# Instance norm on one core: loops without a block, one activation table, and a first store that waits for the third load

## The chip, the cores and the metric

One core of a Trainium2 chip. The metric is the device time of one execution in microseconds, as the profiler takes it. It is 1.7 us longer than the span from the first to the last instruction.

## The reference

```python
x: (8, 64, 32, 64, 64) float32            # 512 instances of 131072 elements
mean = np.mean(x, axis=(2, 3, 4), keepdims=True)
var  = np.var(x, axis=(2, 3, 4), keepdims=True)
out  = (x - mean) / np.sqrt(var + eps)
```

268 MB are read and 268 MB are written; each element is needed once.

## The kernel before

Data moves in 64 tiles of 128 partitions x 8192 floats (4 MiB) through six slots. The last tile is handled as two halves. SyncE issues all loads, ACT issues all stores: one queue for each. A slot is loaded again when its store has landed. The six first loads are issued at once.

```python
def on_scalar(eng, t, lane, n, c1, c2, c16, dst):        # one tile on ACT
    eng.activation(..., func=Act.Identity, accum_out=a[:, 1:2])._wait_ge(landed[lane], c16)
    eng.activation(..., func=Act.Square, bias=a[:, 2:3], accum_out=a[:, 3:4])._wait_ge(centred[lane], c1)
    eng.activation(..., func=Act.Sqrt, bias=eps_t[:, 0:1])._wait_ge(varied[lane], c1)
    eng.activation(out=t[:, :w], func=Act.Identity, scale=a[:, 5:6], bias=a[:, 6:7])._wait_ge(shifted[lane], c1)
    eng.dma_start(out=dst, in_=t)._wait_ge(done[lane], c2).then_inc(stored[lane], 16)
...                                                       # VectorE and TensorE likewise
block = ctx.enter_context(nc.Block())

@block.sync
def _(eng):
    for s in range(SLOTS):
        eng.dma_start(out=slots[s][:], in_=x_t[s]).then_inc(landed[s], 16)
    ...
    with eng.Fori(1, ROUNDS) as it:
        for s in range(SLOTS):
            eng.dma_start(out=slots[s][:], in_=x_t[it * SLOTS + s])._wait_ge(stored[s], c16).then_inc(landed[s], 16)
...
@block.scalar
def _(eng):
    eng.wait_ge(ready, READY)
    over_tiles(eng, on_scalar, with_target=True)          # Fori of 10 passes x 6 tiles, then 5 more
    ...                                                   # ACT waits for all stores
```

## Time and profile before

| | before |
|---|---|
| time, median | 1248.55 us (1248.55, 1248.55, 1250.43) |
| span of the profiled run | 1246.9 us |
| DMA | 431 GB/s over the span, 433 in the middle |
| ACT / DVE busy | 79% / 38% |
| ACT_TABLE_LOAD | 20, two in each loop pass |
| first store issued | 31.85 us |

Read it as a kernel that moves bytes: the engines have slack, and whatever is not plain transfer lies in the first 41 us and the last 24. The lines are in the prediction.

### The profile page before, as it was taken

The page shows a single profiled execution, that of the slowest core. Times are in us where ns is not written, and L with a number is a line of the kernel's source. Part 1 is how long each engine was busy: PE and PEld are TensorE (multiplying, and loading weights), DVE is VectorE, ACT ScalarE, POOL GpSimd, SP SyncE. Part 2 cuts the span into 40 slices and gives each one's busy share as a digit, 9 for nine tenths or more (in the row PEclk, how much of TensorE's full clock was granted, in tenths as well). Part 3 has the DMA queues.
Part 4 walks back from the last instruction along what each step waited for, and adds up shares of the span by engine and source line. Part 5 has one row for each costly group of instructions (what it writes and reads, how often), then busy time and mean ns, then how long its engine had stood idle before and what let it go on. Part 6 is the DMA issues. An engine that isn't in the chain of part 4 may idle for free.

```text
span 1246.9 us, 1819 instructions
## 1 busy us (share of the span) xinstructions
PE 76.4 (6%) x260; PEld 65.2 (5%) x260; DVE 467.9 (38%) x325; ACT 986.1 (79%) x410; POOL 1.9 (0%) x11
## 2 busy tenths in 40 slices
PE   0000000000000000000000000000000000000000
PEld 0000000000000000000000000000000000000000
DVE  2344334433334334343343433433334333343331
ACT  5888888887787878778777878787787878778774
POOL 0000000000000000000000000000000000000000
DMA  9999999999999999999999999999999999999998
GB/s 403 422 435 427 433 436 435 428 433 436 435 428 433 437 434 429 432 436 435 431 430 436 436 434 425 437 436 435 427 434 436 435 428 433 436 435 428 433 432 376
DMA packets 18723, 536.90 MB, mean 431 GB/s; under 512 B 2081, under 2 KB 2081, under 8 KB 2081
## 3 DMA queue, kind: packets, MB, share of 16 engines
q1 hardware_dynamic: 9360, 268.44, 50.0%
q10 hardware_dynamic: 9360, 268.44, 49.9%
q14 instruction: 3, 0.02, 0.0%
HBM read 268.44 MB, written 268.44 MB: 431 GB/s over the span
## 4 chain that ended last, share of the span: by engine, by line
ACT 48%; DVE 29%; another core or an unknown queue 13%; PE 6%; issue 1%; DMA 1%; ACTq 0%; DVEq 0%; SPq 0%
ACT unused L113 37%; DVE small L79 18%; DVE slot L95 8%; ACT slot L123 4%; ACT unused L107 4%; PE psum L136 3%; PE psum L143 3%; ACT small L120 1%; ACT L120 1%; DMA slot<-in_x_dram 1%; DVE small L89 1%; DVE small L82 1%; DVE small L92 1%; ACTq L130 0%
## 5 line engine op out<-in xcount | busy, mean ns | idle before, releaser
L113 ACT ACTIVATE unused<-slot,small 128x8192 uint8<-128x8192 f32 (+1 forms) x65 | 456.1, 7017 | 90.1 <-DVE small L82 90.1
L79 DVE TENSOR_REDUCE small<-slot 128x1 f32<-128x4096 f32 (+1 forms) x65 | 282.9, 4353 | 164.4 <-DMA slot<-in_x_dram 164.4
L107 ACT ACTIVATE unused<-slot 128x4096 uint8<-128x4096 f32 (+1 forms) x65 | 231.7, 3564 | 82.1 <-DMA slot<-in_x_dram 77.0
L123 ACT ACTIVATE slot<-slot,small 128x4096 f32<-128x4096 f32 (+1 forms) x65 | 243.7, 3749 | 27.6 <-DVE small L92 27.6
L89 DVE RECIPROCAL small<-small 128x1 f32<-128x1 f32 x65 | 10.6, 164 | 533.8 <-ACT small L120 533.8
L95 DVE TENSOR_SCALAR slot<-slot,small 128x4096 f32<-128x4096 f32 (+1 forms) x65 | 154.7, 2379 | 2.4
L136 PE MATMUL psum<-small,avg 128*128 128x2 f32 x130 | 38.2, 363 | 674.1 <-DVE small L79 548.7
L136 PEld LDWEIGHTS psum<-small,avg 128*128 128x128 f32 x130 | 32.6, 311 | 679.6 <-DVE small L79 553.0
L143 PE MATMUL psum<-small,avg 128*128 128x1 f32 x130 | 38.2, 363 | 480.6 <-ACT unused L113 480.6
L143 PEld LDWEIGHTS psum<-small,avg 128*128 128x128 f32 x130 | 32.7, 312 | 486.2 <-ACT unused L113 486.2
L120 ACT ACTIVATE small<-psum,eps_t 128x1 f32<-128x1 f32 x65 | 17.0, 261 | 37.4 <-PE psum L143 37.3
L82 DVE TENSOR_REDUCE small<-psum 128x1 f32<-128x2 f32 x65 | 10.3, 159 | 62.5 <-PE psum L136 62.5
L107 ACT ACT_TABLE_LOAD x10 | 12.8, 1283 | 10.4 <-ACT slot L123 7.1
L120 ACT ACT_TABLE_LOAD x10 | 12.8, 1283 | 0.2
L107 ACT ACTIVATION_READ_ACCUMULATOR unused<-slot 128x1 f32 x65 | 12.1, 186 | 0.0
L113 ACT ACTIVATION_READ_ACCUMULATOR unused<-slot,small 128x1 f32 x65 | 12.1, 186 | 0.0
L92 DVE TENSOR_TENSOR small<-small 128x1 f32<-128x1 f32 x65 | 10.3, 159 | 2.2
L208 POOL TENSOR_SCALAR_AFFINE_SELECT avg<-avg 128x128 f32<-128x128 f32 x4 | 1.3, 324 | 0.3
L205 POOL MEMSET avg<- 128x128 f32 x2 | 0.4, 204 | 0.5 <-SPq L42 0.5
L257 POOL MEMSET const-bfloat16-1.0<- 128x1 bf16 x1 | 0.1, 101 | 0.0
L257 POOL MEMSET const-uint8-127<- 128x1 uint8 x1 | 0.1, 101 | 0.0
L257 POOL MEMSET const-float32-0.0<- 128x1 f32 x1 | 0.1, 98 | 0.3 <-issue 0.3
(2 smaller groups left out, 0.2 us busy)
## 6 DMA issues: line engine op xcount, KB each, us to landing
slot<-in_x_dram SPq DMA_DIRECT2D x63, 4096.0 KB, 52.8
out_dram<-slot ACTq DMA_DIRECT2D x63, 4096.0 KB, 45.3
slot<-in_x_dram SPq DMA_DIRECT2D x2, 2048.0 KB, 55.6
out_dram<-slot ACTq DMA_DIRECT2D x2, 2048.0 KB, 14.7
```

The source lines that it names most:

```text
L79: eng.reduce_sum(out=a[:, 0:1], in_=t[:, :w], axis=mybir.AxisListType.X)._wait_ge(landed[lane], c16).then_inc(summed[lane], 1)
L82: eng.tensor_reduce(out=a[:, 2:3], in_=psum[lane][:, 0:2], axis=mybir.AxisListType.X, op=Alu.add, negate=True,)._wait_ge(meaned[lane], c1) ...
L89: eng.reciprocal(out=a[:, 5:6], in_=a[:, 4:5])._wait_ge(rooted[lane], c1).then_inc(scaled[lane], 1)
L92: eng.tensor_mul(out=a[:, 6:7], in0=a[:, 2:3], in1=a[:, 5:6])._wait_ge(scaled[lane], c1).then_inc(shifted[lane], 1)
L95: eng.tensor_scalar(out=t[:, w:], in0=t[:, w:], scalar1=a[:, 5:6], scalar2=a[:, 6:7], op0=Alu.mult, op1=Alu.add,)._wait_ge(shifted[lane], ...
L107: eng.activation(out=unused[:, w : 2 * w], in_=t[:, w:], func=Act.Identity, accum_out=a[:, 1:2],)._wait_ge(landed[lane], c16).then_inc(sum ...
L113: eng.activation(out=unused[:, : 2 * w], in_=t, func=Act.Square, bias=a[:, 2:3], accum_out=a[:, 3:4],)._wait_ge(centred[lane], c1).then_in ...
L120: eng.activation(out=a[:, 4:5], in_=psum[lane][:, 2:3], func=Act.Sqrt, bias=eps_t[:, 0:1])._wait_ge(varied[lane], c1).then_inc(rooted[lane ...
L123: eng.activation(out=t[:, :w], in_=t[:, :w], func=Act.Identity, scale=a[:, 5:6], bias=a[:, 6:7],)._wait_ge(shifted[lane], c1).then_inc(don ...
L136: eng.matmul(out=psum[lane][:, 0:2], lhsT=avg[n][:], rhs=a[:, 0:2], start=True, stop=True,)._wait_ge(summed[lane], c2).then_inc(meaned[lan ...
L143: eng.matmul(out=psum[lane][:, 2:3], lhsT=avg[n][:], rhs=a[:, 3:4], start=True, stop=True,)._wait_ge(squared[lane], c1).then_inc(varied[la ...
L208: eng.affine_select(out=m[:], in_=m[:], pattern=[[sign * split, n], [0, split]], compare_op=Alu.is_ge, fill=0.0, base=0 if sign < 0 else s ...
```

## The change

The intent: no block, so no entry and exit of one; one activation table loaded ahead, in place of two switches in each loop pass; the first store held until the third load has landed. "Last tile in two halves" is in both kernels.

```diff
+    FIRST_BEHIND = 2
...
+        if lane == 0:
+            eng.wait_ge(landed[FIRST_BEHIND], 16)
         eng.dma_start(out=dst, in_=t)._wait_ge(done[lane], c2).then_inc(stored[lane], 16)
...
-    block = ctx.enter_context(nc.Block())
-    @block.sync
-    def _(eng):
+    def load_all(eng):
...                                            # SyncE now waits for all stores, ACT no longer
+        for lane in range(LANES):
+            eng.wait_ge(stored[lane], 16 * uses)
...
+    load_all(nc.sync)
+    set_by = set_up(nc.gpsimd)
+    over_tiles(nc.vector, on_vector)
+    nc.tensor.wait_ge(ready, set_by)
+    over_tiles(nc.tensor, on_tensor)
+    nc.scalar.preload_act_table(Act.Sqrt)
+    nc.scalar.wait_ge(ready, set_by)
+    over_tiles(nc.scalar, on_scalar, with_target=True)
```

More of the change, by code (lines that the diff above doesn't have):

```diff
@@ L160 @@
         rest.append((x_h[k], out_h[k], half, SLOTS + h, 1, FULL // 2))
+    MATRICES = [(m, n, 1.0 / n_elem) for n, m in avg.items()]
     def over_tiles(eng, step, with_target=False):
@@ L197, in _, with set_up @@
             )
-    @block.gpsimd
-    def _(eng):
+        for lane in range(LANES):
+            uses = sum(1 for r in rest if r[3] == lane) + (ROUNDS if lane < SLOTS else 0)
+            eng.wait_ge(stored[lane], 16 * uses)
+    def set_up(eng):
         count = 0
-        for n, m in avg.items():
+        for m, n, value in MATRICES:
             split = P // n
-            eng.memset(m[:], 1.0 / n_elem).then_inc(ready, 1)
+            eng.memset(m[:], value).then_inc(ready, 1)
             count += 1
@@ L218, in _ @@
         eng.memset(eps_t[:], eps_f).then_inc(ready, 1)
-    READY = 3 * len(avg) + 1
-    @block.vector
-    def _(eng):
-        over_tiles(eng, on_vector)
-    @block.tensor
-    def _(eng):
-        eng.wait_ge(ready, READY)
-        over_tiles(eng, on_tensor)
-    @block.scalar
-    def _(eng):
-        eng.wait_ge(ready, READY)
-        over_tiles(eng, on_scalar, with_target=True)
-        for s in range(SLOTS):
-            uses = ROUNDS + sum(1 for r in rest if r[3] == s)
-            eng.wait_ge(stored[s], 16 * uses)
-        for s in range(SLOTS, LANES):
-            eng.wait_ge(stored[s], 16)
+        return count + 1
+    load_all(nc.sync)
[6 more added lines that the diff above has]
+    over_tiles(nc.scalar, on_scalar, with_target=True)
 _INS = ['x', 'eps']
```

## The prediction

> **What bounds the kernel now.** I first read the page, by slices, then the groups, to see whether an engine or the DMA sets the time:
>
> ```profile
> span 1246.9 us, 1819 instructions
> PE 76.4 (6%) x260; PEld 65.2 (5%) x260; DVE 467.9 (38%) x325; ACT 986.1 (79%) x410; POOL 1.9 (0%) x11
> ...
> DMA  9999999999999999999999999999999999999998
> HBM read 268.44 MB, written 268.44 MB: 431 GB/s over the span
> ```
>
> The DMA row is 9 in 39 of 40 slices, and ACT, the busiest engine, is idle a fifth of the time. The chain that ended last names ACT for 48%, but that chain follows releases backwards and does not say what is full. I therefore cut the span into stages. The columns are stretch, its length, busy time of PE, PEld, DVE, ACT and POOL, clock, DMA share, GB/s:
>
> ```profile
> 0.00:2.05 2.05, 0.00 (x0) 0.00 (x0) 0.00 (x0) 0.00 (x0) 1.09 (x8) 1.00 0.00 0
> 2.05:31.50 29.45, 1.18 (x4) 1.01 (x4) 8.38 (x6) 17.23 (x8) 0.80 (x4) 1.00 1.01 427
> 31.50:41.20 9.70, 0.59 (x2) 0.50 (x2) 3.42 (x2) 8.35 (x4) 0.00 (x0) 1.00 1.02 402
> 41.20:116.20 75.00, 5.28 (x18) 4.51 (x18) 30.45 (x23) 64.34 (x28) 0.00 (x0) 1.00 1.00 432
> 116.20:1180.90 1064.70, 65.20 (x222) 55.71 (x222) 407.44 (x278) 854.27 (x352) 0.00 (x0) 1.00 1.00 433
> 1180.90:1223.40 42.50, 2.94 (x10) 2.51 (x10) 14.07 (x13) 33.73 (x16) 0.00 (x0) 1.00 1.00 432
> 1223.40:1243.20 19.80, 1.17 (x4) 1.00 (x4) 4.11 (x5) 8.16 (x6) 0.00 (x0) 1.00 0.98 423
> 1243.20:1245.40 2.20, 0.00 (x0) 0.00 (x0) 0.00 (x0) 0.00 (x0) 0.00 (x0) 1.00 0.05 22
> 1245.40:1246.90 1.50, 0.00 (x0) 0.00 (x0) 0.00 (x0) 0.00 (x0) 0.00 (x0) 1.00 0.00 0
> ```
>
> From 2 us to 1243 us the DMA engines are full, at 433 GB/s for the long middle. All 536.9 MB at 433 GB/s are 1239.9 us, so only about 7.0 us of the span are not plain transfer. The table says where they lie, each as length x (1 - rate/433): 2.05 before the first packet, 0.41 in the ramp, 0.69 in the stage where the first store joins the loads (31.5 to 41.2), about 0.3 in the middle and the drain of the loads, 0.46 while the last stores run alone, 2.09 while the last DMA engine finishes, 1.50 of waits and barriers after it. That is 7.5 us with rounded rates. **A change that moves no fewer bytes can only win inside these pieces.**
>
> Whether a queue ever runs dry is the next question. The stores, by line, and the waits of ACT:
>
> ```profile
> L130 ACTq DMA_DIRECT2D out_dram<-slot x65: 338/338/397, 31.9 to 1233.9; - x65
> ...
> DMA to landing us min/median/max: 11.4/45.3/46.1
> ```
> ```profile
> ACT unused L107 <- DMA slot<-in_x_dram: 77.0, 44, 8.9
> ```
>
> One tile in and out is 8.39 MB, 19.4 us at 433 GB/s, yet a store lands 45.3 us after its issue: about two stores are queued. Loads take 52.8 us to land, so they are queued as well. ACT waits for a load in 44 of 65 tiles. The engines have slack and both queues always have work.
>
> **What the Trainium skill says.** "DMA: Bandwidth & Descriptors", section "Where 436 GB/s comes from", gives 435.2 GB/s as the fabric's ceiling; the trace shows 433 in the middle, half a per cent below, so the middle has nothing to give. The same page, "Issuing engines are not separate DMA queues", says that transfers of all issuing engines run on the same 16 DMA engines and interleave; the trace agrees: adding the store queue to the load queue left the rate at 432 to 433 (432 before, over 11.7 to 31.1 us). "ScalarE: Activation LUTs", section "What ACT_TABLE_LOAD costs", gives some 1283 ns a load plus a drain of about 1380 ns for each switch. The trace has 1283 ns, but the Sqrt begins 1.30 us after its load begins, so no such drain shows here.
>
> **The change, part by part.** In all parts the bytes, tiles, slots, reductions and matmuls stay the same.
>
> *Head without a block.* Each engine now enters its program by a branch (SyncE's at 0.9 us, 37 ns long), and SyncE's first load is issued at 1.03 us:
>
> ```profile
> 1.03 2.95 SPq L183 DMA_DIRECT2D slot<-in_x_dram  x6
> ...
> 3.31 1.28 ACT L107 ACT_TABLE_LOAD   x1 [3.31 <-POOL eps_t L218]
> ...
> 26.04 1.28 ACT L120 ACT_TABLE_LOAD   x1
> 27.34 0.26 ACT L120 ACTIVATE small<-psum,eps_t 128x1 f32<-128x1 f32 x1
> ...
> 31.85 0.40 ACTq L130 DMA_DIRECT2D out_dram<-slot  x1
> ```
>
> If the branch goes, the first load can be issued at the branch's place, 0.86 us in the trace: -0.17 us, and all of it counts, because every later packet follows on a full queue.
>
> *Tail without a block.* The last store's semaphore is full at 1245.35 us. Now ACT passes its wait, branches (1245.44), drains (1245.61), and all engines pass the block's barrier (until 1245.83) before SyncE starts the outer exit:
>
> ```profile
> _compat.py:109 ACTq COMPARE_BRANCH  x1: 38/38/38, 1245.4 to 1245.4; - x1
> _compat.py:109 ACTq DRAIN  x1: 8/8/8, 1245.6 to 1245.6; - x1
> _compat.py:109 SPq EVENT_SEMAPHORE  x1: 17/17/17, 1245.8 to 1245.8; - x1
> ```
>
> After the change SyncE itself waits for the stores and goes straight to the outer exit: it would start at about 1245.44 in place of 1245.84, so -0.40 us. The outer exit's barriers, 1.0 us, stay.
>
> *One activation table.* The page has 10 + 10 table loads of 1.283 us, two per loop pass: 25.7 us of ACT. Preloading Sqrt's table leaves one, since the second to sixth tile of each pass already run Identity and Square after Sqrt without a reload. That frees about 24 us of ACT, but ACT is not the bound: worth 0 on the path. The one place where it touches the path's timing is tile 0. The Sqrt there would start when its matmul ends (26.7 us in the trace) and not at 27.34: the first store would be ready 0.64 us sooner, at 31.2.
>
> *First store behind the third load.* The first load releases ACT at 13.51 us, and a load alone takes 4.194 MB / 432 GB/s = 9.7 us. The third thus lands at 13.5 + 19.4 = 32.9 us, 0.17 less with the earlier head. The first store goes out at about 32.8, not 31.85: one microsecond later. ACT stands meanwhile, so tile 1's sum starts at about 33.2 instead of 32.29. The load queue has three more loads in it and keeps the DMA engines full, so the delay swaps the order of bytes and loses none: 0. In the loop's later passes the wait is already met; it costs ACT some tens of ns (its other waits take 17 to 38 ns), in slack.
>
> *Last tile in two halves.* Both kernels have this already: 0.
>
> Sum: -0.17 - 0.40 = -0.57 us on the span. The measured time is 1.65 us over the span (1248.55 against 1246.9), which I keep. 1248.55 - 0.57 = 1247.98, and I lean down slightly for the join below: **1247.9 us**.
>
> **Rivals.**
>
> *The table loads were on the path.* For it: 79% of ACT, and 37% of the chain is the Square pass. If ACT were the bound, 24 us less would give 1224.5. Against it: the DMA share is 1.00 in each middle stage, and a store released 2.6 us sooner only stands longer in a queue 45 us deep.
>
> *The later first store shifts the whole chain of stores.* If stores ran one by one with no backlog, the end would move by the microsecond that the first waits: about 1249.0. Against it: loads move in its place, and in the tail the last store is issued at 1233.9 while the one before it lands only at 1240.5; it has work ahead of it.
>
> *The join gets cheaper or dearer.* The stage in which the first store joins loses 0.69 us. If the packets fall better when the store starts at a load's end, up to 0.7 us is won (1247.3); if the 16 engines fall out of step, as much may be lost (1248.7). The last store's sixteen increments in the trace come at 1243.2 to 1245.3, one engine a microsecond after the fifteenth, so the slowest engine sets the end, and the phase given to it at the start may stay to the end. I see nothing that decides the sign; I give 0.1 us to the author's intent.
>
> *Loops outside a block cost something new*, for instance a barrier or an instruction fetch at each pass. Against it: the loops are the same instructions per engine, and now one back edge on ACT takes well under a microsecond (branch at 119.25, next move at 119.51). Even 2 us ten times on ACT would be hidden behind the queues: the span would change by under 1 us.
>
> **Range and chances.** The sure part is 0.57 us. The join and the spread of the 16 engines may move it by some 0.7 us either way, and three runs of before spread by 1.9 us upwards (1248.55 to 1250.43), which a median of a few may catch. So 1246.6 to 1249.3. A 2% gain would need 25 us, more than three times all that is not transfer: 1%. A 2% loss needs the DMA to stand for 25 us: 1%.
>
> **What would show each step.** Head: the first load's issue at about 0.86 us and first packets at about 1.9. Tail: 1.1 us, not 1.5, from the last increment to the end. Tables: one ACT_TABLE_LOAD, ACT busy near 961 us. Join: first store at about 32.8 us, and the stage's loss still near 0.7 us. Middle: 433 GB/s. I am wrong if the rate of the middle changes, if table loads stay in the loop (then the ACT figure is wrong, the time is not), if a queue runs dry in the tail, or if the spread of the last increments grows or shrinks by more than a microsecond.

## The result, and the profile after

| | before | after |
|---|---|---|
| executions, us | 1248.55, 1248.55, 1250.43, 1248.70 | 1249.45, 1249.65, 1249.54, 1249.75 |
| median | 1248.62 | 1249.60 |
| span of the profiled run | 1246.9 | 1247.7 |

The ratio is 1.0004 (0.9987 to 1.0022): the same within 2%. A ratio is the mean time of one kernel's fast runs over that of the other's of the same rounds, so not quite the ratio of the medians; here the 1250.43 lifts the mean of before. Executions over 1.5% slower than the fastest of the same kernel are left out of the means. By the medians the changed kernel is 1.0 us slower, where 0.6 us faster was forecast, and its median lies 0.3 us above the range. The interval includes 1, so the times alone don't show that it is slower: all four executions of it lie above three of before's and below the fourth. The traces show where the microsecond goes.

From the page of the changed kernel, its span, the busy times, and the only table load that is left:

```profile
span 1247.7 us, 1790 instructions
PE 76.3 (6%) x260; PEld 65.2 (5%) x260; DVE 467.9 (37%) x325; ACT 961.7 (77%) x391; POOL 1.9 (0%) x11
...
L232 ACT ACT_TABLE_LOAD x1 | 1.3, 1283 | 1.0 <-SPq L43 1.0
```

ACT does 24 us less. The same stages as in the prediction (stretch, length, busy times, clock, DMA share, GB/s):

```profile
31.50:41.20 9.70, 0.58 (x2) 0.50 (x2) 2.72 (x2) 6.87 (x3) 0.00 (x0) 1.00 0.99 385
...
116.20:1180.90 1064.70, 65.19 (x222) 55.69 (x222) 408.62 (x278) 833.65 (x334) 0.00 (x0) 1.00 1.00 433
...
1223.40:1243.20 19.80, 1.17 (x4) 1.00 (x4) 2.88 (x5) 6.93 (x6) 0.00 (x0) 1.00 0.99 425
1243.20:1245.40 2.20, 0.00 (x0) 0.00 (x0) 0.00 (x0) 0.00 (x0) 0.00 (x0) 1.00 0.09 37
1245.40:1247.70 2.30, 0.00 (x0) 0.00 (x0) 0.00 (x0) 0.00 (x0) 0.00 (x0) 1.00 0.00 0
```

The middle keeps its 433 GB/s. What differs is the last line and the one above it: the end is later by 0.8 us. The branches and the issues of the changed kernel, by line and from the timeline, show what became of the head and the exit:

```profile
L265 SPq COMPARE_BRANCH  x1: 33/33/33, 0.9 to 0.9; - x1
```
```profile
L198 SPq COMPARE_BRANCH  x1: 37/37/37, 1246.5 to 1246.5; - x1
```
```profile
1.02 2.95 SPq L186 DMA_DIRECT2D slot<-in_x_dram  x6
...
33.02 0.40 ACTq L135 DMA_DIRECT2D out_dram<-slot  x1
```

The branch at the head is still there, and the first load goes out at 1.02 us, not 0.86. One branch is left at the exit too. A transfer's semaphore gets sixteen increments in the trace, read here as one from each DMA engine at the end of its share. From the last increment of the last store to the end it takes 1.30 us (1246.44 to 1247.74) where before took 1.55 (1245.35 to 1246.89).

So 0.25 us were won at the exit and 1.10 us were lost ahead of it. The loss sits in the last of the sixteen increments. The sixteen increments of the last store, from the trace's records of them, in us:

```
          first     median    15th      16th
before    1243.24   1243.49   1244.38   1245.35
after     1243.27   1243.50   1244.39   1246.44
```

In order of time, the first, the median and the fifteenth come within 0.03 us of where they came before (some between them move by up to 0.4 us). The sixteenth is 1.1 us later. I had named "the phase given to it at the start" as something I could not size. The experiments therefore take the change apart and move the first store, and with it the moment at which its packets come between those of the loads (the join).

### The profile page after: what moved, and what is told of

Same layout as the page of the kernel before. It is cut to its first block, busy times and chain, and to the rows that moved or that the text cites. A ratio compares the mean times of both kernels' runs of the same rounds, so it can differ in the third digit from the quotient of the medians.

```text
span 1247.7 us, 1790 instructions
## 1 busy us (share of the span) xinstructions
PE 76.3 (6%) x260; PEld 65.2 (5%) x260; DVE 467.9 (37%) x325; ACT 961.7 (77%) x391; POOL 1.9 (0%) x11
## 4 chain that ended last, share of the span: by engine, by line
DMA 49%; another core or an unknown queue 29%; ACT 15%; DVE 3%; PE 1%; SPq 1%; issue 1%; ACTq 0%
DMA slot<-in_x_dram 26%; DMA out_dram<-slot 23%; ACT unused L114 8%; ACT slot L124 4%; DVE small L80 2%; ACT unused L108 2%; PE psum L148 1%; PE psum L141 1%; SPq L191 1%; ACT small L121 0%; ACTq L135 0%; DVE small L90 0%; DVE small L83 0%; DVE small L93 0%
## 5 line engine op out<-in xcount | busy, mean ns | idle before, releaser
L232 ACT ACT_TABLE_LOAD x1 | 1.3, 1283 | 1.0 <-SPq L43 1.0
```

## The experiments

Two theories at the outset. **Mine:** the time at which the first store joins the loads decides how much single DMA engines lose, and nothing else in the change matters but the 0.25 us at the exit. **The rival:** the wait costs what it delays, because the stores form the chain that ends last.

### Four kernels on one chip: parts of the change, and a later first store

**e1_no_wait** is the changed kernel without the wait.

```diff
-        if lane == 0:
-            eng.wait_ge(landed[FIRST_BEHIND], 16)
```

> The changed kernel without the wait of the first store for the third load; block and tables as changed. My theory (one DMA engine ends late: it lost 1.7 us where the first store joined the loads instead of 0.9, and adds its own steady drift): the first store goes out at about 31.2 us, the joins fall on other engines' packets, so the last increment moves by up to a microsecond either way from 1246.4; the exit still takes 1.29 us from the last increment. Which way is not derived. Rival (the wait itself delays the chain of stores by the 1.8 us it holds the first store): the span falls by about 1.8 us, to 1245.9, and all sixteen increments of the last store come earlier, not one alone.

Measured: 1258.55, 1257.06, **1286.43**, 1259.90, 1256.94, **1285.79** us; the two in bold are slow, and no trace of them was kept. The four fast ones have the median 1257.8, ratio to before 1.0074 (1.0059 to 1.0089). Both theories fail in size, and the rival in sign. Taking the wait away costs 8 us against the changed kernel.

**e2_block_and_wait** is the kernel before with the wait alone.

```diff
+        if lane == 0:
+            eng.wait_ge(landed[2], 16)
         eng.dma_start(out=dst, in_=t)._wait_ge(done[lane], c2).then_inc(
```

> The kernel before with the wait alone added; block and table loads kept. My theory: the bulk of the last store's increments stay at 1243.2 to 1244.4, the sixteenth moves with the join; exit 1.55 us. If the join falls as in the changed kernel, the last increment is near 1246.4 and the span 1248.0. Rival (the wait costs its own delay): first store about 1.1 us later than in before, all increments of the last store 1.1 us later, span 1248.0 too, so the increments and not the time tell them apart.

Measured: 1249.77 to 1249.87 us, median 1249.83 (before beside it 1248.57). The last store's increments: median 1243.53, fifteenth 1244.35, sixteenth 1246.61. All stay within 0.2 us of before's except the last, so the wait is not paid as a delay. It makes one engine late, as in the changed kernel. (The ratio's interval, 0.9996 to 1.0022, includes 1 because one execution of before, of eleven, took 1250.36; the ten others end at 1248.89.)

**e3_wait_for_fourth** has `FIRST_BEHIND = 3` in the changed kernel.

> The changed kernel with the first store behind the fourth load, about 42.5 us, 9.7 us later than in the changed kernel. My theory: the loads fill the time, the fifteen other increments stay within 0.4 us of 1243.3 to 1244.4, and the time stays within 1.5 us of the changed kernel. Rival (delay of the first store is paid): span up by about 9.7 us, to 1257.

Measured: 1248.98, 1256.51, 1250.18, 1248.92, 1249.06, 1249.98 us, median 1249.52. The first store goes out at 42.6 us, 9.6 us later than in the changed kernel, and the time is the same: the rival falls. One execution in six was 7 us longer.

**e4_one_table** is the kernel before with the preloaded table alone.

```diff
     def _(eng):
+        eng.preload_act_table(Act.Sqrt)
         eng.wait_ge(ready, READY)
```

> The kernel before with the preloaded table alone. One table load in place of 20, ACT busy near 962 us, the first store 0.64 us earlier at 31.2. My theory: 24 us of ACT are worth 0 in the bulk of the increments (1243.2 to 1244.4); the sixteenth may move by up to a microsecond with the join. Rival (tables on the path): over 2% faster.

Measured: 1257.93 to 1259.83 us, median 1258.89, ratio 1.0082 (1.0069 to 1.0095). **Less work on ACT makes the kernel 10 us slower.** No increment was as expected.

In e1 and e4 the first store goes out only 0.8 to 0.95 us sooner than in before. From the timelines of e1 and then of e4:

```profile
30.90 0.40 ACTq L131 DMA_DIRECT2D out_dram<-slot  x1
```
```profile
31.07 0.40 ACTq L130 DMA_DIRECT2D out_dram<-slot  x1
```

The stages of e1 from 116 us on (the last stretch was asked for up to 1260 and ends at the span's end, 1256.8):

```profile
116.20:1180.90 1064.70, 64.58 (x220) 55.16 (x220) 399.96 (x276) 822.09 (x331) 0.00 (x0) 1.00 1.00 432
...
1223.40:1243.20 19.80, 2.35 (x8) 2.00 (x8) 5.50 (x9) 14.37 (x12) 0.00 (x0) 1.00 0.83 357
1243.20:1260.00 16.80, 0.00 (x0) 0.00 (x0) 1.39 (x2) 2.09 (x1) 0.00 (x0) 1.00 0.37 157
```

The middle loses 1 GB/s in 433, which looks harmless. It is a mean over sixteen engines, and it hides the cause. The increments of one late load (slot 1, tenth pass), each against the first of the sixteen, in us:

```
before  0 0.03 0.08 0.24 1.02 1.04 1.06 1.09 1.24 1.27 1.30 1.32 1.32  1.56  1.77  2.76
e1      0 0.01 0.06 0.10 0.14 0.16 0.18 0.19 0.36 0.91 1.86 6.83 9.84 10.20 10.69 12.49
e4      0 0.01 0.01 0.02 0.11 0.13 0.13 0.15 0.18 0.24 0.57 1.01 2.12  6.98 11.29 11.44
```

In e1 five engines, in e4 three, have fallen 7 to 12 us behind. A tile is only complete when the slowest has its share. The last load is complete at 1234.9 us in place of 1223.5, and ACT's timeline in e1 shows the rest of the story:

```profile
1234.95 1.91 ACT L108 ACTIVATE unused<-slot 128x2048 uint8<-128x2048 f32 x1 [0.86 <-DMA slot<-in_x_dram]
...
1245.40 0.34 ACTq L131 DMA_DIRECT2D out_dram<-slot  x1
```

From there 10.5 us of arithmetic and a store follow with nothing to hide them: the DMA is at 357 GB/s in this stage where before had 423.

What sets an engine apart? The trace names no engine for a packet, but packets of one engine follow each other to a few ns, so the sixteen strings can be rebuilt. Below, from about 26 us on, L is a load packet (32 KiB), S a store packet, l and s the increment that ends the engine's share of a load or a store, and a number in brackets the ns that a packet took over the usual 1213. Where engines stand within a few ns of each other, which packet belongs to which is not unique.

```
before         LLLLlLLL(508)SL(214)SLSLSLSLSlSLSLsLSLSLSLSLSLSlSLSLsLSLSL
after          LLLLlLLL(720)L(249)SLSLSLSLSlSLSLSLsLSLSLSLSLSlSLSLSLsLSLSL
e1, 11 such    LLLLlLL(125)L(856)SLSLSLSLSLSlSLSLsLSLSLSLSLSLSlSLSLsLSLSLS
e1, 5 such     LLLLLlLL(560)SLSLSLSLSLSLSlSLsL(367)SLSLSL(40)SLSLSLSlS(25)LsL(303)SLSLSL
```

The two queues take turns packet by packet. The Trainium skill says so ("DMA: Bandwidth & Descriptors", section "Queues, rings and completion order": each DMA engine goes round robin between the queues at packet granularity), and the trace agrees, with one row of 32 KiB as a packet. As every tile has eight packets on each engine in both queues, **the order of l and s that the first store finds is repeated for the whole run.** In the five slow engines the first store came after 2 load packets of the current load, and s follows l by 2 packets each time; the packet after it takes 0.2 to 0.4 us too long. In the eleven others the first store came after 3, s follows l by 4, and nothing is lost. In e4 three engines had 2, and three are slow. In before it was 3 (twelve engines) and 4 (four); in after 4 (thirteen) and 5; in e2 4 in all sixteen.

That is the new theory, the **phase theory**: an engine is slow when a store's increment closely follows a load's on it. Its rival: a first store ahead of the third load's landing is bad as such. Before speaks against that already, with 31.85 us and the landing at 32.1 to 32.9.

### Four kernels that move the first store through one load's period

POOL, idle otherwise, holds the first store. K fills of 512 columns start when the third load has landed:

```diff
+    go, ticks = semaphores("go", 2)
+    spin = sbuf("spin", [P, 512])
...
-            eng.wait_ge(landed[FIRST_BEHIND], 16)
+            eng.wait_ge(go, 1)
...                                            # on POOL, after its set-up
+        eng.wait_ge(landed[FIRST_BEHIND], 16)
+        for i in range(K):
+            eng.memset(spin[:], 0.0)._wait_ge(ticks, i).then_inc(ticks, 1)
+        eng.memset(spin[:, 0:1], 0.0)._wait_ge(ticks, K).then_inc(go, 1)
```

> The changed kernel, the first store held by a chain of 12 idle fills on POOL that starts when the third load has landed, so issued near 40 us. Phase theory (from e1 and e4: an engine is slow for the whole run if it had moved 2 load packets of the current load when the first store's packets joined; the 5 and 3 slow engines there were the 5 and 3 with 2): 40.1 is one load of 9.7 us after 30.4, so most engines join at 2 packets and the time is bad again, 1255 us or more; if all sixteen are slow, the rate of the whole middle falls below 430 GB/s. Rival (bad because the store goes out before the third load has landed): like the changed kernel, 1249 to 1250.

> As before with 10 fills, first store near 38.9 us: the engines join at about 1 packet. Phase theory as found so far says slow at 2 and nothing of 1; I guess slow too, 1255 or more. Rival (before the third load only): 1249 to 1250.

> 8 fills, first store near 37.7 us, joining at about 0 or 8 packets: the ends of the load and of the store would then fall together on each engine. Phase theory: open, 1249 to 1265. Rival: 1249 to 1250.

> 4 fills, first store near 35.3 us, joining at about 6 packets, far from 2. Both theories: 1249 to 1250.5, with a spread of the last increments of 2 to 4 us.

Measured, with the runs so far in the order of the first store's place in the 9.7 us of a load ("2 x12" means that twelve engines had moved 2 load packets when the store joined):

| kernel | first store, us | load packets ahead of it | time, us |
|---|---|---|---|
| e6, K = 10 | 39.0 | 1 or less x11, 2 x5 (one engine uncertain) | 1254.8 (one run 1266.0, the one traced) |
| e5, K = 12 | 40.0 | 2 x12, 3 x4 | **1286.3** (1285.0 to 1287.2) |
| e1 / e4 | 30.9 / 31.1 | 2 x5 / 2 x3, others 3 | 1257.8 (fast runs) / 1258.9 |
| before | 31.85 | 3 x12, 4 x4 | 1248.6 |
| e2 / after | 32.8 / 33.0 | 4 x16 / 4 x13, 5 x3 | 1249.8 / 1249.6 |
| e3 | 42.6 | 4 x10, 5 x6 | 1249.5 |
| e8, K = 4 | 35.5 | 6 x16 | 1249.3 |
| e7, K = 8 | 37.6 | 8 or more x9, 1 x7 | 1249.6 |

e5 decides it. Its first store is 9 us later than e1's, long after the third load, and stands at nearly the same place in the load's period (0.6 us earlier, with more engines at 2). It is 3% slower than before (ratio 1.030, 1.028 to 1.032). That e1's two slow executions have the same 1286 us is not explained by any trace. Here the whole middle is slower; e5's stages, and then e8's middle:

```profile
41.20:116.20 75.00, 5.29 (x18) 4.52 (x18) 29.05 (x21) 64.56 (x27) 0.00 (x0) 1.00 1.01 422
116.20:1180.90 1064.70, 64.02 (x218) 54.69 (x218) 395.65 (x273) 816.29 (x328) 0.00 (x0) 1.00 1.00 426
1180.90:1223.40 42.50, 2.35 (x8) 2.01 (x8) 15.79 (x11) 32.51 (x13) 0.00 (x0) 1.00 1.00 423
```
```profile
116.20:1180.90 1064.70, 65.78 (x224) 56.21 (x224) 408.88 (x280) 836.24 (x337) 0.00 (x0) 1.00 1.00 433
```

The strings give the condition more finely. For each distance between the two increments, counted in data packets over the first three tiles after the join, the mean ns lost on the packets around one such pair (e6 is traced in its 1266 us execution, and its figures depend most on how the strings are rebuilt):

```
s after l by 0    e6 105, e7 23
s after l by 2    e1 253, e4 243, e5 386, e6 125
s after l by 4    before 0, e1 0, e4 5          (e5's four engines: 513)
s after l by 6    before 21, after 0, e2 0, e3 0
s after l by 8    after 0, e3 0
l after s by 6    e8 0
l after s by 2    e7 0
```

A load's increment that follows a store's by 2 costs nothing; a store's that follows a load's by 2 costs 0.13 to 0.39 us each time in these runs. Two points do not fit a rule for single engines. In e5 the four engines at distance 4 lose as much as the twelve at 2, so slow engines seem to hold up others. And e7's seven engines at distance 0 lose little and the run stays good, while e6, with eleven at 0 or 1 and five at 2, is 6 us slow in the median and 17 us in the execution traced.

### The block alone, the last engine, the records, and the order shifted on purpose

**e9_no_block_only** is the changed kernel without preload and without wait.

```diff
-            eng.wait_ge(landed[FIRST_BEHIND], 16)      # and its "if lane == 0:"
-    nc.scalar.preload_act_table(Act.Sqrt)
```

> The changed kernel with neither the preloaded table nor the wait: what is left of the change is the loops without a block. 20 table loads come back, the first store is ready at 31.85 us as in before, so each engine joins at 3 or 4 load packets and none should be slow. Expected: like before in all but the exit, 1.29 us from the last increment in place of 1.55, so 1248.3. If the block part itself had cost the microsecond that the changed kernel shows over before, it would be 1249.6.

Measured: 1248.17 to 1248.41 us, median 1248.23, beside 1248.53 for before. The exit takes 1.30 us in place of 1.55, as forecast, and the last increment is at 1245.26, 0.08 us sooner than in before. This is the fastest kernel, by 0.3 us in the median; its interval (0.9982 to 1.0010) includes 1, since before has one execution of nine at 1250.15.

**e10_spare_engine** cuts the last store of e9 in two.

```diff
+        if lane == LANES - 1:
+            eng.dma_start(out=dst[0:120], in_=t[0:120])._wait_ge(done[lane], c2).then_inc(stored[lane], 16)
+            eng.dma_start(out=dst[120:128], in_=t[120:128]).then_inc(extra, 16)
+            return
```

> The same, and the very last store cut into rows 0 to 119 and 120 to 127, which leaves the sixteenth DMA engine without a share in it (if the cut goes over the engines as I assume) and gives eight others one packet of 0.61 us more. One engine ends about 1 us after all others in each good run. If it is the sixteenth, the end comes 0.5 to 1 us sooner, 1247.5; if it is one of the first eight, 0.6 us later, 1248.9; else unchanged.

Measured: median 1251.91 us (1251.83 to 1254.13), 3.7 us slower than e9, outside all three cases. One of the sixteen increments comes at 1234.6, at once, as the Trainium skill's rule for 120 rows on 15 engines says (same page, "Why a DMA increments its semaphore by 16 and not by 1"). But the median increment moves from 1243.5 to 1245.6 and the last to 1248.2 and 1248.8. One increment of the larger part still comes 1.8 us after the one before it, so the late engine is probably not the one left out; but the others moved too, and this is not settled. The cut itself costs, and why is not shown.

**e11_pool_records** adds to before, on POOL:

```diff
+        with eng.Fori(0, 400):
+            for _ in range(40):
+                eng.reg_mov(idle, 5)
```

> The kernel before with 16000 register moves on idle POOL, which use no memory. One DMA engine falls behind the rest by some 0.03 us a tile in every run. If that comes from writing the records of executed instructions (1819 of them in before), nine times as many make it fall behind much faster while POOL is busy, 5 us or more, and the time rises by as much. If it comes from elsewhere: 1248.5, the same drift.

Measured: 1249.08 us. **Inconclusive**: the trace holds 2620 instructions, not some 18000, so most of the moves were not executed or not recorded. With 44% more records the late engine falls behind by 0.18 us in six tiles, in before by 0.17; the test was too weak to say more.

**e12_shifted_ring** is e1 with half a tile more on the store queue ahead of the first store, once. ACT's first pass is written out for it.

```diff
+        if more:                                       # tile 0 only
+            eng.dma_start(out=out_t[n_tiles - 1][0:64], in_=t[0:64])._wait_ge(done[lane], c2).then_inc(extra, 16)
+        if lane == SLOTS:                              # the last tile overwrites those rows
+            eng.wait_ge(extra, 16)
         eng.dma_start(out=dst, in_=t)._wait_ge(done[lane], c2).then_inc(
```

> The changed kernel without the wait, so with the first store at the bad time of about 31.1 us as in e1, but half a tile (4 packets for each engine) goes out on the store queue just ahead of the first store, once; ACT's first pass is written out for that. It goes to rows that the last tile overwrites later. Phase theory (slow when a store's increment follows a load's by 0 or 2 packets on the same engine): all later ends of stores move 4 packets away, no engine is slow, the middle runs at 433 GB/s; 2.1 MB more take 4.8 us, so 1253 to 1254. Rival (a first store at 31.1 us is bad in itself, whatever follows it): e1's 1257 to 1259 plus 4.8, 1262 to 1264, with slow engines as in e1.

Measured: 1255.44 to 1255.71 us, median 1255.62. The store queue starts at 31.18 us, 0.1 us after e4's, and no engine is slow: the sixteen increments of the same late load as above spread over 2.9 us. The issue of the half tile and the stages of e12:

```profile
31.18 0.56 ACTq L133 DMA_DIRECT2D out_dram<-slot  x1
```
```profile
41.20:116.20 75.00, 5.28 (x18) 4.51 (x18) 30.33 (x23) 64.33 (x28) 0.00 (x0) 1.00 1.00 419
116.20:1180.90 1064.70, 64.87 (x222) 55.45 (x222) 407.62 (x277) 830.60 (x333) 0.00 (x0) 1.00 1.00 433
```

The middle is at 433. The time is 1.6 us over my 1254, at least in part because the join itself was dearer: 419 GB/s in the first stretch where before had 432, 75 x (1 - 419/432) = 2.3 us. The rival asked for 1262 or more with slow engines: a first store at 31.2 us is not bad in itself. The run doesn't show that moving the later ends of stores is the cure. In its rebuilt strings all sixteen engines had moved 3 load packets when the half tile joined, none 2, as in e9, whose sixteen at 3 are good without a half tile. By the phase theory this execution would have been good without it too.

## Why the prediction was right or wrong

- **The bound and the rate of the middle: right.** 433 GB/s in both kernels; no gain of percents.
- **Head without a block, -0.17 us: wrong.** The branch stayed; the first load goes out at 1.02 us. I took the only branch for the block's own.
- **Tail without a block, -0.40: right mechanism, size off.** It gave 0.25, because a branch remains there too. e9 shows it nearly alone: 1248.23 against 1248.53.
- **One activation table, 0 on the path: wrong when it stands alone.** The 24 us of ACT indeed bring no gain in any run. But the 0.64 us by which the first store is ready sooner, which I named (0.78 in e4's trace), is what costs 10 us (e4: 1258.9).
- **First store behind the third load, "swaps the order of bytes and loses none": the step that failed.** It swaps the order for the whole run. With the tables kept, the wait costs 1.3 us (e2: 1249.8 against 1248.6). With one table it saves 8 us (after 1249.6, fast runs of e1 1257.8) by moving the join out of the bad place. So the change holds a loss of 8 to 10 us and its cure, and what remains is 1.0 us by the medians; in the profiled runs -0.25 at the exit and +1.10 on the last engine make the span 0.85 longer. That the total came within 1.7 us of the forecast is luck: neither the loss nor the cure stood in the sum. A sign of being wrong that the prediction named did appear: the last store's increments spread over 3.17 us in place of 2.11.
- **The rival "the join gets cheaper or dearer": named, but given 0.7 us.** The join did get dearer: 385 GB/s against 402 in the stage of 9.7 us is 0.4 us more. The lasting part was missing: after the join the late engine of before falls behind by 0.15 to 0.20 us in six tiles, by 0.25 to 0.29 in the changed kernel and by 0.32 to 0.36 in e2, where the increments of most or all engines lie 6 apart in place of 4. In the bad place it is 0.13 to 0.39 us for each pair of increments in the first tiles, and on several engines.

Why a store's increment close behind a load's makes the engine wait is not shown. The Trainium skill says ("Queues, rings and completion order") that an increment "lands only after every earlier write from that SDMA engine, across its queues". Two increments close together with stalls right behind the second fit that, but no run takes the increments away. A rival stands untested: the distance between the increments is also the distance between the rows that the two queues move at the same time, so a conflict between those rows would follow the same pattern. It is also open why one engine falls slowly behind in each good run, why e5 slows engines at a good distance, and what puts before at 1250.2 to 1250.4 in one execution of ten.

## What to carry to other kernels

When two transfer queues run full for a whole kernel and their tiles have equal numbers of packets, look at the moment at which the second queue joins: in these runs it fixed the order of their ends for good. A first store 0.8 us sooner, from an engine that got faster, cost 0.8% (e4), the worst place 3% (e5), and in e1 a mean rate of the middle lower by just 1 GB/s hid it. Compare the spread of a DMA's sixteen increments, early and late in the run, and move the join by a wait whose place you choose.

## What the Trainium skill lacked or had wrong

- "DMA: Bandwidth & Descriptors", "Queues, rings and completion order": it has the round robin and the ordered increments, but not that the distance between two queues' increments matters. Measured: 1248.6 us at 3 to 4 load packets ahead of the first store, 1286.3 us with twelve of sixteen engines at 2.
- The same page, "Where 436 GB/s comes from", says that for transfers between HBM and SBUF the HBM side at about 358 GB/s binds. Here one core ran 433 GB/s of loads and stores for over a millisecond, close to the 435 of the fabric. The passage lacks the condition that the page gives elsewhere, in its note on single-core numbers (under "Measured (HBM→SBUF, 128 partitions, SWDGE, issued from GpSimd)"): about 358 each when both cores of an HBM domain stream.
- The same page, "Specifications", gives a first byte after about 0.6 us for queues such as these. The first load, issued at 1.03 us, shows its first packet at 2.05; the first store, issued at 31.85 while the loads ran, at 35.95. What fills these 4.1 us is not shown.
- "ScalarE: Activation LUTs", "What ACT_TABLE_LOAD costs": the load's 1283 ns agree; the drain of about 1380 ns does not show here, the Sqrt begins 1.30 us after the load begins.
- "ScalarE activation tables: per-element evaluation and per-set limits", "Table sets in the compiler and the runtime", says that the table loads are placed per block. It lacks what that does to a loop: two reloads in each pass, although five tiles of six run all functions under Sqrt's table, and that one table loaded ahead of the loop removes them all (20 loads before, 1 after).
